# Attention in a hybrid decoder layer: turned probabilities kept in float32, each value product split by head parity onto the two halves of TensorE's columns

## The chip, the core and the metric

The kernel runs on one core of a Trainium2 chip. A core has TensorE (PE in the profile, with its loads of weights in a row of their own, PEld), VectorE (DVE), ScalarE (ACT), GpSimd (POOL) and SyncE (SP, which issues the DMAs). Tiles lie in SBUF, with 128 partitions; TensorE writes its results to PSUM, 8 banks of 2 KB a partition. The metric is the device time of one execution in microseconds, lower is better.

## What is computed

One layer of a decoder trunk on a sequence of 1024 tokens with 1024 features. The input is normalized and projected; eight heads of sparse attention (two groups of four heads of width 64, each group with one set of keys and values) and four heads of a gated delta rule work side by side, their outputs go through one projection and a residual addition, and a gated feed-forward part with a short convolution follows. The change lies in the attention. For every block of queries it forms three softmaxes and their products with values:

```python
p_cmp = masked_softmax(jnp.einsum('bqhgd,bhnd->bhgqn', qb, kc), m_cmp)      # 64 compressed keys
o_cmp = jnp.einsum('bhgqn,bhnd->bqhgd', p_cmp, vc)
...
p_sel = masked_softmax(jnp.einsum('bqhgd,bhqnd->bhgqn', qb, k_sel), m_sel[:, :, None])
o_sel = jnp.einsum('bhgqn,bhqnd->bqhgd', p_sel, v_sel)                      # selected blocks of keys
...
p_win = masked_softmax(jnp.einsum('bqhgd,bkhd->bhgqk', qb, kw), m_win)
o_win = jnp.einsum('bhgqk,bkhd->bqhgd', p_win, vw)                          # a window of 512
...
return jnp.einsum('bshc,bshcd->bshd', gate, o)                              # gated sum of the three
```

Everything is float32. The output is the layer's result after a last normalization.

## The kernel before

The program runs through four stages. `phase_in` normalizes, projects and runs the delta rule (0 to about 455 us in the trace); `phase_attend` does the attention and the part of the output projection that does not need it (to about 790); `phase_out` and `norm_second` finish the projection and the second normalization; `phase_up` and `phase_down` are the feed-forward part (from about 820).

TensorE takes float32 operands in two ways. Operands of the type float32r are rounded on writing, and one instruction multiplies them in one pass. Precision is kept by splitting a tile into a rounded high part and the rounded rest (`wh`, `wl`; `hH`, `hL`; `qh`, `ql`) and summing products of the parts in PSUM; `mm3` does so with three products. Operands of the type float32 are multiplied in full, and the trace shows two MATMUL and two LDWEIGHTS instructions for each such product. The delta rule uses these, for instance `kk_ps` (L285): 128 rows, 64 columns of weights, written by turns to partitions 0 to 63 and 64 to 127 of one PSUM tile. A transposition on TensorE takes float32 tiles and shows one instruction.

The attention works in 16 **units**: a tile of 128 queries `i` (in the order 7 to 0) and a group `g` of four heads. Each unit passes three generators. `select` forms the scores of the compressed keys (`sc_ps`) and picks the blocks. `scores` forms for each head the window scores and the scores of all earlier keys (`s_ps`, L820 and L822: high and low part of the queries against `kst`, whose 128 rows hold the high and the low part of the keys), adds masks and finds maxima on VectorE (L834), takes the exponential on ScalarE (L838) and scales by gate and sum on POOL (L854); the results are `pw` (`p_win`) and `pn` (`p_sel`). `values` (L867) sums all three value products of the unit in one PSUM tile `po`. It goes through a list of jobs: one for the 64 compressed keys, one for each 128 keys of the window (at most 5) and one for each 128 keys up to the query tile, 148 jobs over all units. A job turns the probabilities of the four heads with four transposes into the PSUM tile `pt` (L880; three buffers, shared with `og_ps`), and then:

```python
nc.scalar.activation(ph[0:kk], pt[0:kk], AF.Copy)                                       # L882: high part
...
nc.vector.tensor_tensor(out=pl, in0=pt, in1=ph.bitcast(F32), op=ALU.subtract)           # L890: the rest
nc.tensor.matmul(po, v, ph, start=False, stop=False)                                    # L891
nc.tensor.matmul(po, v, pl, start=False, stop=(n == len(jobs) - 1))                     # L892
```

The weights `v` (`K.vst`, L601) are 128 rows of keys by 128 columns, the high part of the 64 value features and beside it their low part; so `po` holds the products with the high part in partitions 0 to 63 and those with the low part in 64 to 127, 512 columns wide (four heads of 128 queries). The job of the compressed keys (L885, L886) has its 64 rows twice, the high and the low part of the probabilities below each other. At the end of a unit the two halves of `po` are copied out and added into `oT`, in which heads of even number lie in partitions 0 to 63 and of odd number in 64 to 127: for `i` under 4 one copy on ScalarE and two additions on VectorE (L897, L899), otherwise two copies on ScalarE and two additions on POOL (L904, L906). `nsa_norm` takes `oT` from there.

`K.vst` is made at the end of `phase_in`: four loads of `v_raw` from DRAM (L611), four rounding copies on ScalarE (L613) and four subtractions on POOL (L614). `K.vc` is made in `compress` with four copies on ScalarE and four subtractions on VectorE (L717, L718).

`interleave` (L92) mixes the generators of three neighbouring units and `out_gdn`, the output projection of the delta rule's part (`og_ps`, twelve products of 512 columns for a tile). That sets only the order in which the program is written: the tile framework runs it through a scheduler with a timeline of its own, which sets the order on each engine. Each engine then works through its order in turn.

Of the kernel before, what the change touches and what calls it, by code (L numbers as in the profile page):

```python
# [9 lines left out]
F32 = mybir.dt.float32  # L10
F32R = mybir.dt.float32r
BF16 = mybir.dt.bfloat16
AF = mybir.ActivationFunctionType
ALU = mybir.AluOpType
# [494 lines left out]
def phase_in(K, ctx):  # L509
# [91 lines left out]
    K.vst = vp.tile([P, NT, 2, 2, P], F32R, name="vst")  # L601
# [6 lines left out]
    vr = scr.enter_context(tc.tile_pool(name="vraw", bufs=4, side="right"))  # L608
    for j in range(4):
        raw = vr.tile([P, 2, 2, 2, 64], F32, name="v_raw", tag="v_raw")  # L610
        nc.sync.dma_start(raw.rearrange("p t b g d -> p t (b g d)"), K.d_v[:, 2 * j:2 * j + 2, :])  # L611
        d = slice(2 * j, 2 * j + 2)
        nc.scalar.activation(K.vst[:, d, :, :, 0:64], raw, AF.Copy)  # L613
        nc.gpsimd.tensor_tensor(out=K.vst[:, d, :, :, 64:128], in0=raw, in1=K.vst[:, d, :, :, 0:64].bitcast(F32),  # L614
                                op=ALU.subtract)
# [46 lines left out]
def compress(K, which, pool):  # L662
# [47 lines left out]
    else:  # L710
        for h in range(2):
            vp = K.pp.tile([64, 64], F32, name="vc_ps", tag="proj")
            for j in range(2):
                nc.tensor.matmul(vp, x[:, j, 64 * h:64 * h + 64], w2[:, j, :], start=(j == 0), stop=(j == 1))

            for d in (slice(0, 64), slice(64, 128)):
                nc.scalar.activation(K.vc[d, h, 0:64], vp, AF.Copy, scale=0.5)  # L717
                nc.vector.scalar_tensor_tensor(out=K.vc[d, h, 64:128], in0=vp, scalar=0.5,  # L718
                                               in1=K.vc[0:64, h, 0:64].bitcast(F32), op0=ALU.mult, op1=ALU.subtract)
# [147 lines left out]
def values(K, i, g, U):  # L867

    nc = K.nc
    pc, pw, pn, lo = U.pc, U.pw, U.pn, U.lo  # L870
    po = K.p_o.tile([P, 4, P], F32, name="po", tag="po")
# [5 lines left out]
    for n, (src, v, kk) in enumerate(jobs):  # L877
# [3 lines left out]
        ph = K.apl.tile([P, 4, P], F32R, name="ph", tag="ph", bufs=3)  # L881
        nc.scalar.activation(ph[0:kk], pt[0:kk], AF.Copy)  # L882
        if n == 0:

            nc.vector.tensor_tensor(out=ph[kk:P], in0=pt[0:kk], in1=ph[0:kk].bitcast(F32), op=ALU.subtract)  # L885
            nc.tensor.matmul(po, v, ph, start=True, stop=False)  # L886
            yield
            continue
        pl = K.apl.tile([P, 4, P], F32R, name="pl", tag="pl", bufs=3)
        nc.vector.tensor_tensor(out=pl, in0=pt, in1=ph.bitcast(F32), op=ALU.subtract)  # L890
        nc.tensor.matmul(po, v, ph, start=False, stop=False)  # L891
        nc.tensor.matmul(po, v, pl, start=False, stop=(n == len(jobs) - 1))  # L892
        yield

    if i < 4:
        lo_ = K.apl.tile([64, 4, P], F32, name="po_s", tag="po_s", bufs=1)
        nc.scalar.activation(lo_, po[64:128], AF.Copy)  # L897
        for par in range(2):
            nc.vector.tensor_tensor(out=U.oT[64 * par:64 * par + 64, 2 * g:2 * g + 2, :], in0=po[0:64, par::2, :],  # L899
                                    in1=lo_[:, par::2, :], op=ALU.add)  # L900
        return
    hh = K.apl.tile([64, 2, 4, P], F32, name="po_s", tag="po_s", bufs=1)
    for j in range(2):
        nc.scalar.activation(hh[:, j], po[64 * j:64 * j + 64], AF.Copy)  # L904
    for par in range(2):
        nc.gpsimd.tensor_tensor(out=U.oT[64 * par:64 * par + 64, 2 * g:2 * g + 2, :], in0=hh[:, 0, par::2, :],  # L906
                                in1=hh[:, 1, par::2, :], op=ALU.add)
# [512 lines left out]
def open_common(K, ctx):  # L1420
# [22 lines left out]
    K.vc = cp.tile([P, 2, P], F32R, name="vc")  # L1443
# [103 lines left out]
```

## Time and profile before

| | us |
|---|---|
| median of 3 runs | 1500.02 (1499.13 to 1500.04) |
| the profiled execution, its own time | 1502.3 |
| its span, first to last instruction | 1500.5 |
| first transpose of probabilities to last value product | 502.8 to 790.4 |

The profile is of one execution. Its times are microseconds, ns where said. A busy share is the time in which an engine has at least one instruction under way; matmuls overlap each other, so it says little of how full TensorE is. A row of the timeline is a start, a duration, engine and line, operation, the tile written and the tiles read, the form (rows by columns of the weights, then partitions by columns of the moving tile) and how many like it stand in a row; the duration of a row of several runs from the first start to the last end. A releaser ("<-") is what an idle engine was waiting for.

### The profile page before, as it was taken

To read this page: it belongs to the slowest core of one execution; us is meant where nothing else is said; L and a number is where in the kernel's file an instruction comes from. 1 tells how busy PE (TensorE), PEld (TensorE's weight loads), DVE (VectorE), ACT (ScalarE), POOL (GpSimd) and SP (SyncE) were. 2 spreads that over 40 slices of the span, in tenths; PEclk is the share of its full clock that TensorE was granted. 3 is DMA by queue.
4 is the path that set the end of the run, shared out by engine and by line. 5 is a ranking of instruction groups with operands and counts; after the bars stand their busy time and mean duration, and the time that the engine had idled before them with its cause. 6 is when DMAs were issued, how large, how long until landed. Compare 5 with 4: busy or idle time off the path is not lost.

```text
span 1500.5 us, 21074 instructions
## 1 busy us (share of the span) xinstructions
PE 1420.9 (95%) x7260; PEld 1163.8 (78%) x7260; DVE 1153.7 (77%) x2222; ACT 723.3 (48%) x1405; POOL 575.3 (38%) x567
## 2 busy tenths in 40 slices
PE   8998899999989999989998979999999999989997
PEld 8876677787877777777787858888888888778886
DVE  5768997886335788898975797888888888687656
ACT  7443343232233566788865544444444445333333
POOL 3355433344352245466563541111111112364444
PEclk9999999999999999999999989999999999999999
DMA  6245352444366543132215112323222235773333
GB/s 234 87 156 177 107 169 72 125 121 150 93 219 173 161 138 112 58 85 52 55 64 200 40 70 105 105 105 106 105 94 98 97 105 194 268 267 87 103 106 147
DMA packets 106059, 188.04 MB, mean 125 GB/s; under 512 B 17216, under 2 KB 52064, under 8 KB 105952
## 3 DMA queue, kind: packets, MB, share of 16 engines
q1 hardware_dynamic: 105952, 186.69, 38.5%
q8 instruction: 57, 0.93, 0.3%
q14 instruction: 50, 0.41, 0.1%
HBM read 135.00 MB, written 51.66 MB: 124 GB/s over the span
## 4 chain that ended last, share of the span: by engine, by line
PE 64%; DVE 19%; DMA 6%; ACT 4%; issue 4%; POOL 2%; SPq 1%; DVEq 0%; ACTq 0%; POOLq 0%
PE up_ps L1130 27%; PE dn_ps L1328 11%; PE proj_ps L128 3%; PE proj_ps L126 3%; PE proj_ps L127 3%; DVE cv_acc L465 3%; PE pt L880 2%; DVE pl L890 2%; PE po L892 1%; DVE zb L350 1%; PE po L891 1%; DVE ztmp L348 1%; PE s_ps L820 1%; PE s_ps L415 1%; DMA d_x<-og 1%
## 5 line engine op out<-in xcount | busy, mean ns | idle before, releaser
L1328 PE MATMUL dn_ps<-d_op 128*128 128x512 f32 x924 | 211.4, 390 | 5.7 <-DVE d_op L1322 3.8
L1328 PEld LDWEIGHTS dn_ps<-d_op 128*128 128x128 f32 x924 | 173.0, 188 | 43.6 <-DVE d_op L1322 5.0
L128 PE MATMUL proj_ps<-hH,w_l 128*128 128x512 f32 x384 | 158.3, 412 | 6.6 <-POOL w_l L118 6.6
L126 PE MATMUL proj_ps<-hH,w_h 128*128 128x512 f32 x384 | 156.2, 408 | 5.0 <-ACT cv_acc L463 3.2
L127 PE MATMUL proj_ps<-hL,w_h 128*128 128x512 f32 x384 | 155.3, 405 | 0.1
L1320 POOL TENSOR_TENSOR d_op<-a_raw,d_op 128x1024 fp32r<-128x1024 f32 (+1 forms) x42 | 104.7, 2496 | 123.0 <-ACT d_op L1319 105.6
L1130 PE MATMUL up_ps<-th,op_h 128*128 128x512 f32 x336 | 133.5, 398 | 7.1 <-ACT op_h L1154 7.1
L1130 PE MATMUL up_ps<-th,op_l 128*128 128x512 f32 x336 | 133.6, 398 | 3.6 <-DVE op_l L1156 3.6
L1130 PE MATMUL up_ps<-tl,op_h 128*128 128x512 f32 x336 | 133.3, 397 | 0.0
L118 POOL TENSOR_TENSOR w_l<-w_raw,w_h 128x1024 fp32r<-128x1024 f32 (+2 forms) x46 | 110.1, 2398 | 46.1 <-ACT w_h L116 44.5
L1322 DVE TENSOR_TENSOR d_op<-b,d_op 128x1024 fp32r<-128x1024 f32 (+1 forms) x42 | 80.8, 1928 | 48.5 <-ACT d_op L1321 42.1
L1130 PE MATMUL up_ps<-dl,op_h 128*128 128x512 f32 x288 | 113.8, 395 | 0.0
L1130 PE MATMUL up_ps<-dh,op_h 128*128 128x512 f32 x288 | 112.6, 395 | 1.0 <-ACT acc L167 1.0
L1130 PE MATMUL up_ps<-dh,op_l 128*128 128x512 f32 x288 | 110.5, 394 | 0.0
L882 ACT ACTIVATE ph<-pt 128x512 fp32r<-128x512 f32 (+1 forms) x148 | 85.3, 591 | 49.1 <-PE pt L880 41.3
L1242 DVE SCALAR_TENSOR_TENSOR ga<-f_g,vec,ga 128x1024 f32<-128x1024 f32 x44 | 89.3, 2029 | 16.9 <-ACT ga L1240 16.3
L890 DVE TENSOR_TENSOR pl<-pt,ph 128x512 fp32r<-128x512 f32 x132 | 89.5, 683 | 9.1 <-ACT ph L882 8.6
L128 PEld LDWEIGHTS proj_ps<-hH,w_l 128*128 128x128 f32 x384 | 74.6, 194 | 26.9 <-POOL w_l L118 10.6
L1154 ACT ACTIVATE op_h<-w_raw 128x1024 fp32r<-128x1024 f32 (+1 forms) x64 | 59.0, 923 | 74.8 <-PE up_ps L1130 69.7
L1319 ACT ACTIVATE d_op<-a_raw 128x1024 fp32r<-128x1024 f32 (+1 forms) x42 | 41.4, 988 | 108.7 <-PE dn_ps L1328 53.8
L1175 POOL MEMSET f_u<- 128x2 f32 x22 | 2.2, 100 | 234.0 <-DVE acc L1242 233.1
L126 PEld LDWEIGHTS proj_ps<-hH,w_h 128*128 128x128 f32 x384 | 74.6, 195 | 21.2 <-ACT cv_acc L463 4.9
(343 smaller groups left out, 3654.6 us busy)
## 6 DMA issues: line engine op xcount, KB each, us to landing
w_raw<-in_w_up_dram SPq DMA_DIRECT2D x44, 512.0 KB, 3.2
a_raw<-d_a SPq DMA_DIRECT2D x35, 512.0 KB, 3.6
w_raw<-in_w_gdn_dram SPq DMA_DIRECT2D x24, 512.0 KB, 3.5
d_a<-ga SPq DMA_DIRECT2D x44, 256.0 KB, 2.0
b<-in_w_down_dram SPq DMA_DIRECT2D x20, 512.0 KB, 6.9
d_a<-so SPq DMA_DIRECT2D x33, 256.0 KB, 2.0
qT<-d_q SPq DMA_DIRECT2D x32, 256.0 KB, 4.8
mg<-d_mix SPq DMA_DIRECT2D x16, 512.0 KB, 3.7
```

The source lines that it names most:

```text
L118: (low or nc.gpsimd).tensor_tensor(out=wl, in0=raw, in1=wh.bitcast(F32), op=ALU.subtract)
L126: nc.tensor.matmul(out, ah, bh, start=(i == 0), stop=False)
L127: nc.tensor.matmul(out, ah, bl, start=False, stop=False)
L128: nc.tensor.matmul(out, al, bh, start=False, stop=(i == n - 1))
L882: nc.scalar.activation(ph[0:kk], pt[0:kk], AF.Copy)
L890: nc.vector.tensor_tensor(out=pl, in0=pt, in1=ph.bitcast(F32), op=ALU.subtract)
L1130: mm = lambda a, b, start, stop: nc.tensor.matmul(out, a, b, start=start, stop=stop, skip_group_check=not first)
L1154: nc.scalar.activation(h, src, AF.Copy)
L1242: nc.vector.scalar_tensor_tensor(out=a, in0=raw[:, j:j + SEQ], scalar=tap(j), in1=a, op0=ALU.mult, op1=ALU.add)
L1320: nc.gpsimd.tensor_tensor(out=al, in0=raw, in1=ah.bitcast(F32), op=ALU.subtract)
L1322: nc.vector.tensor_tensor(out=bl, in0=b[js.start], in1=bh.bitcast(F32), op=ALU.subtract)
L1328: one = lambda a, b, start, stop: nc.tensor.matmul(ps, a, b, start=start, stop=stop, skip_group_check=not first)
```

## The change

The probabilities are no longer split. `pt` is copied once to a float32 tile `pT`, by VectorE in every fourth job (`n % 4 == 3`) and by ScalarE in the others. The values stay float32 as well: `K.vst` is loaded from DRAM by one DMA with nothing done to it, `K.vc` takes one copy a group. `po` becomes a tile of 256 columns: the heads of even number are multiplied into its partitions 0 to 63, those of odd number into 64 to 127, each with the same 64 columns of values as weights, so that it has the layout of `oT` and is copied there by one instruction on ScalarE.

```diff
-    K.vst = vp.tile([P, NT, 2, 2, P], F32R, name="vst")
+    K.vst = vp.tile([P, NT, 2, 2, 64], F32, name="vst")
+    nc.sync.dma_start(K.vst.rearrange("p t b g d -> p t (b g d)"), K.d_v)
...
-    vr = scr.enter_context(tc.tile_pool(name="vraw", bufs=4, side="right"))
-    for j in range(4):
-        raw = vr.tile([P, 2, 2, 2, 64], F32, name="v_raw", tag="v_raw")
-        nc.sync.dma_start(raw.rearrange("p t b g d -> p t (b g d)"), K.d_v[:, 2 * j:2 * j + 2, :])
-        d = slice(2 * j, 2 * j + 2)
-        nc.scalar.activation(K.vst[:, d, :, :, 0:64], raw, AF.Copy)
-        nc.gpsimd.tensor_tensor(out=K.vst[:, d, :, :, 64:128], in0=raw, in1=K.vst[:, d, :, :, 0:64].bitcast(F32),
-                                op=ALU.subtract)
...
-            for d in (slice(0, 64), slice(64, 128)):
-                nc.scalar.activation(K.vc[d, h, 0:64], vp, AF.Copy, scale=0.5)
-                nc.vector.scalar_tensor_tensor(out=K.vc[d, h, 64:128], in0=vp, scalar=0.5,
-                                               in1=K.vc[0:64, h, 0:64].bitcast(F32), op0=ALU.mult, op1=ALU.subtract)
+            nc.scalar.activation(K.vc[:, h], vp, AF.Copy, scale=0.5)
...
-    po = K.p_o.tile([P, 4, P], F32, name="po", tag="po")
+    po = K.p_o.tile([P, 2, P], F32, name="po", tag="po")
...
-        ph = K.apl.tile([P, 4, P], F32R, name="ph", tag="ph", bufs=3)
-        nc.scalar.activation(ph[0:kk], pt[0:kk], AF.Copy)
-        if n == 0:
-
-            nc.vector.tensor_tensor(out=ph[kk:P], in0=pt[0:kk], in1=ph[0:kk].bitcast(F32), op=ALU.subtract)
-            nc.tensor.matmul(po, v, ph, start=True, stop=False)
-            yield
-            continue
-        pl = K.apl.tile([P, 4, P], F32R, name="pl", tag="pl", bufs=3)
-        nc.vector.tensor_tensor(out=pl, in0=pt, in1=ph.bitcast(F32), op=ALU.subtract)
-        nc.tensor.matmul(po, v, ph, start=False, stop=False)
-        nc.tensor.matmul(po, v, pl, start=False, stop=(n == len(jobs) - 1))
+        pT = K.apl.tile([P, 4, P], F32, name="pT", tag="pT", bufs=4)
+        if n % 4 == 3:
+            nc.vector.tensor_copy(pT[0:kk], pt[0:kk])
+        else:
+            nc.scalar.activation(pT[0:kk], pt[0:kk], AF.Copy)
+        for par in range(2):
+            nc.tensor.matmul(po[64 * par:64 * par + 64], v, pT[0:kk, par::2], start=(n == 0), stop=(n == len(jobs) - 1))
         yield
-
-    if i < 4:
-        lo_ = K.apl.tile([64, 4, P], F32, name="po_s", tag="po_s", bufs=1)
...
+    nc.scalar.activation(U.oT[:, 2 * g:2 * g + 2, :], po, AF.Copy)
...
-    K.vc = cp.tile([P, 2, P], F32R, name="vc")
+    K.vc = cp.tile([64, 2, 64], F32, name="vc")
```

The scheduler makes a new order. On TensorE in the first third of the stage (`pt` are transposes of four heads, `po` value products, `s_ps` scores of the next unit), before:

```order
L880 MATMUL pt<-ident,p_win 128x128 x8
L891 MATMUL po<-ph,vst 128x512
L892 MATMUL po<-pl,vst 128x512
L880 MATMUL pt<-ident,p_sel 128x128 x4
L891 MATMUL po<-ph,vst 128x512
L820 MATMUL s_ps<-kst_4413,qT 128x384
L822 MATMUL s_ps<-kst_4413,qT 128x384
L820 MATMUL s_ps<-kst_4413,qT 128x256
L822 MATMUL s_ps<-kst_4413,qT 128x256
L892 MATMUL po<-pl,vst 128x512
```

and in the changed kernel at the same place:

```order
L872 MATMUL pt<-ident,p_win 128x128 x8
L879 MATMUL po<-pT,vst 64x256 x2
L872 MATMUL pt<-ident,p_sel 128x128 x4
L879 MATMUL po<-pT,vst 64x256 x2
L872 MATMUL pt<-ident,p_sel 128x128 x4
L809 MATMUL s_ps<-kst_4407,qT 128x384
L811 MATMUL s_ps<-kst_4407,qT 128x384
L879 MATMUL po<-pT,vst 64x256 x2
L872 MATMUL pt<-ident,p_sel 128x128 x4
```

The two products of a job, which stood apart with scores between them, now stand together, between transposes or scores of full width. Over all units the 296 value products stand in 129 places.

On ScalarE at the end of `phase_in` (`q_h` is the rounded part of the queries, `w_h` of weights, `wq` the delta rule's output), before:

```order
L643 ACTIVATE q_h<-proj_ps 128x512
L116 ACTIVATE w_h<-w_raw 128x1024 x2
L643 ACTIVATE q_h<-proj_ps 128x512
L613 ACTIVATE vst<-v_raw 128x8x64 x4
L643 ACTIVATE q_h<-proj_ps 128x512
```

and changed:

```order
L636 ACTIVATE q_h<-proj_ps 128x512 x2
L443 ACTIVATE wq<-zT 128x4x128
L636 ACTIVATE q_h<-proj_ps 128x512
L116 ACTIVATE w_h<-w_raw 128x1024 x2
L636 ACTIVATE q_h<-proj_ps 128x512
```

The copies into `vst` between the last two `q_h` are gone; on SP the one load of `vst` stands some eight DMAs earlier than the four loads of `v_raw` stood.

## Rows read from the trace of the kernel before

**Rows 1.** The page's busy time: us (share of the span) x instructions.
```profile
PE 1420.9 (95%) x7260; PEld 1163.8 (78%) x7260; DVE 1153.7 (77%) x2222; ACT 723.3 (48%) x1405; POOL 575.3 (38%) x567
```
**Rows 2.** Windows: length; busy us (count) of PE, PEld, DVE, ACT, POOL; PEclk; DMA.
```profile
502.80:790.40 287.60, 267.96 (x1591) 222.73 (x1589) 247.14 (x808) 211.32 (x537) 149.44 (x217) 0.99 0.30 86
```
**Rows 3.** PE's groups in that stretch: count | busy us, mean ns | idle before.
```profile
L892 PE MATMUL po<-pl,vst 128*128 128x512 f32 x132 | 57.5, 436 | 7.1 <-DVE pl L890 6.8
L891 PE MATMUL po<-ph,vst 128*128 128x512 f32 x132 | 55.8, 423 | 2.0 <-ACT ph L882 2.0
L880 PE MATMUL pt<-ident,p_sel 128*128 128x128 f32 x288 | 44.9, 277 | 1.8 <-DVE og L952 1.8
L880 PE MATMUL pt<-ident,p_win 128*128 128x128 f32 x240 | 36.4, 274 | 5.8 <-DVE pl L890 2.9 <-DVE ph L885 1.6 <-DVE og L952 1.3
L126 PE MATMUL og_ps<-w_h,mg 128*128 128x512 f32 x72 | 29.3, 407 | 0.1
...
L820 PE MATMUL s_ps<-kst,qT 128*128 128x512 f32 x48 | 22.0, 459 | 1.0 <-DVE nmax L834 1.0
L820 PE MATMUL s_ps<-kst,qT 128*128 128x384 f32 x49 | 19.2, 391 | 0.0
...
L820 PE MATMUL s_ps<-kst,qT 128*128 128x256 f32 x50 | 15.7, 320 | 0.0
```
**Rows 4.** Timeline of PE around 654 us: start, duration, line, tiles, form, count.
```profile
654.41 0.40 PE L892 MATMUL po<-pl,vst 128*128 128x512 f32 x1
654.64 0.39 PE L891 MATMUL po<-ph,vst 128*128 128x512 f32 x1
654.87 0.60 PE L880 MATMUL pt<-ident,p_sel 128*128 128x128 f32 x4
655.23 0.30 PE L820 MATMUL s_ps<-kst,qT 128*128 128x128 f32 x1
```
**Rows 5.** Timeline of PE around 109 us, in the delta rule.
```profile
109.21 0.39 PE L127 MATMUL proj_ps<-hL,w_h 128*128 128x512 f32 x1
109.53 1.09 PE L285 MATMUL kk_ps<-kq 128*64 128x128 f32 x16
110.55 0.50 PE L128 MATMUL proj_ps<-hH,w_l 128*128 128x512 f32 x1
110.89 0.40 PE L126 MATMUL proj_ps<-hH,w_h 128*128 128x512 f32 x1
```
**Rows 6.** Timeline of PE around 301 us (`ot_ps` are transposes).
```profile
300.35 0.60 PE L437 MATMUL ot_ps<-ident,vv 128*128 128x128 f32 x4
300.88 0.44 PE L285 MATMUL kk_ps<-kq 128*64 128x128 f32 x4
301.25 0.66 PE L437 MATMUL ot_ps<-ident,vv 128*128 128x128 f32 x4
```
**Rows 7.** By tile: ns shortest/median/longest, first and last start in us.
```profile
L270 PE MATMUL nd_ps<-ug,cst x8: 590/592/697, 80.6 to 287.0; 128*128 128x512 f32 x8
...
L285 PE MATMUL kk_ps<-kq x128: 272/273/324, 109.5 to 302.4; 128*64 128x128 f32 x128
```
**Rows 8.** PE's waits from 502.8 to 790.4 us, the first and the last: total, times, longest.
```profile
PE po L892 <- DVE pl L890: 6.8, 8, 1.9
...
PE po L886 <- DVE oT L899: 0.2, 1, 0.2
```
**Rows 9.** The page's groups of `ph` and `pl`: busy us, mean ns | idle before.
```profile
L882 ACT ACTIVATE ph<-pt 128x512 fp32r<-128x512 f32 (+1 forms) x148 | 85.3, 591 | 49.1 <-PE pt L880 41.3
...
L890 DVE TENSOR_TENSOR pl<-pt,ph 128x512 fp32r<-128x512 f32 x132 | 89.5, 683 | 9.1 <-ACT ph L882 8.6
```
**Rows 10.** The chain that ended last, at 438 us: start, duration.
```profile
438.64 5.63 DMA v_raw<-d_v
```
**Rows 11.** PE's waits from 455 to 810 us, one row.
```profile
PE sc_ps L744 <- DMA qT<-d_q: 1.6, 1, 1.6
```
**Rows 12.** Timeline of PE at 420 us.
```profile
420.88 0.79 PE L126 MATMUL proj_ps<-hH,w_h 128*128 128x512 f32 x1 [1.58 <-DVE vc L718]
```

More of the change, by code (lines that the diff above doesn't have):

```diff
@@ L880, in values @@
             nc.tensor.transpose(pt[0:kk, h, :], src[h], K.ident)
-        ph = K.apl.tile([P, 4, P], F32R, name="ph", tag="ph", bufs=3)
-        nc.scalar.activation(ph[0:kk], pt[0:kk], AF.Copy)
-        if n == 0:
-            nc.vector.tensor_tensor(out=ph[kk:P], in0=pt[0:kk], in1=ph[0:kk].bitcast(F32), op=ALU.subtract)
-            nc.tensor.matmul(po, v, ph, start=True, stop=False)
-            yield
-            continue
-        pl = K.apl.tile([P, 4, P], F32R, name="pl", tag="pl", bufs=3)
-        nc.vector.tensor_tensor(out=pl, in0=pt, in1=ph.bitcast(F32), op=ALU.subtract)
-        nc.tensor.matmul(po, v, ph, start=False, stop=False)
-        nc.tensor.matmul(po, v, pl, start=False, stop=(n == len(jobs) - 1))
-        yield
-    if i < 4:
-        lo_ = K.apl.tile([64, 4, P], F32, name="po_s", tag="po_s", bufs=1)
[L897 to L907, printed above, removed]
+        pT = K.apl.tile([P, 4, P], F32, name="pT", tag="pT", bufs=4)
[5 more added lines that the diff above has]
+            nc.tensor.matmul(po[64 * par:64 * par + 64], v, pT[0:kk, par::2], start=(n == 0), stop=(n == len(jobs) - 1))
+        yield
+    nc.scalar.activation(U.oT[:, 2 * g:2 * g + 2, :], po, AF.Copy)
 def nsa_norm(K, i, o):
```

## The prediction

> **What bounds the kernel now.** By the page's busy shares PE is busy 95% of the span [rows 1]. A busy share does not say how full PE is, so I cut out the stage that the change touches, from the first probability transpose (502.8) to the last value product (790.4): 287.6 us, in which PE is busy 268 us and VectorE 247 us [rows 2]. The question is whether PE's own work fills the stage or whether PE waits for VectorE's `pl`. I counted PE's instructions there by shape [rows 3] and took from the timeline how far apart they start when nothing is in the way: a rounded (float32r) product of 512 columns takes its place for 0.23 us (the two value products start at 654.41 and 654.64), a transpose for 0.11 us (four last 0.60, a single one 0.27, so three steps are 0.33), and the step to the next operation costs next to nothing [rows 4]. Then, in us: 592 transposes (528 in the rows, 64 of `pc` by the code) x 0.11 = 65; 280 value products (132 `pl`, 132 `ph` and 16 of the compressed values by the code) x 0.23 = 64; 217 products of `og` (three rows of 72 or 73, of which one stands) x 0.23 = 50; score products, each row having a twin for the low part, 96 x 0.23 = 22, 98 at 384/512 of that = 17, 100 at half = 11; about 200 small ones at 0.11 or less, 19. That is 249 of 287.6. **PE is 87% full there, and 38 us are left for waits**, of which the waits list names 18.6 us in nine rows, the longest for `pl` [rows 8]. So VectorE can give back at most 38 us; anything over that would have to come off PE.
>
> **What the change takes away.** VectorE loses 132 `pl` at 683 ns [rows 9], 90 us, 16 half-height ones and 16 final additions. It gets the copy of every fourth job (n = 3, 7, 11 in a unit: 30 in all), at most 0.68 each like `pl`, the nearest row that reads as much from PSUM: 20 us. So its 247 fall to under 177. ScalarE loses those 30 copies and the ones of `po_s`. Neither ends this stage afterwards. What PE gains is waits only: nearly all of the 18.6 us named are for `pl`, `ph` or for an `og` addition that stands behind `pl` on VectorE, so I let 18 go and keep 20 of the 38 (late first score maxima, ScalarE behind a weight's DMA, the clock at 0.99 [rows 2]). Ends for what stays: 0 and 38.
>
> **What the change puts on PE.** Each job had two rounded products of 512 columns, 0.46 us. Now it has two true float32 products of 256 columns, into partitions 0 to 63 and 64 to 127 of `po`. Three terms, each from work of the same kind elsewhere in this trace.
> First, the rate. A float32 product appears as two passes (the trace counts 16 where the order has 8). A pass of 512 columns lasts 592 ns and one of 128 lasts 273 [rows 7]; (592-273)/384 = 0.83 ns a column. So a pass of 256 columns takes 0.21 us, and the four of a job, one after the other, would take 0.85.
> Second, whether the halves run together. `kk_ps` is the row to go by: float32, 64 columns of weights, the same two halves in turn. From the end of L127 (109.60) to the end of `kk_ps` (110.62) are 1.02 us for 16 passes of 128 columns [rows 5]; at 0.107 each they would need 1.71. They run in pairs: 8 x 0.107 = 0.86, and 0.16 is left over. So a job is two paired steps, 0.43 us, against 0.46 (0.23 in the first job of a unit): 148 x 0.43 = 64 against 64. **The arithmetic is a draw.**
> Third, the switch. The 0.16 is what PE pays to go from full width to halves: `kk_ps` starts 0.32 after L127, not 0.23, and its first passes last up to 324 ns, not 273 [rows 5, 7]. Coming back, L128 ends 0.43 after `kk_ps` instead of 0.23: 0.20 [rows 5]. Between transposes it is the same: from the end of the first four (300.95) to the end of the next four (301.91) are 0.96 us, for 0.21 of paired passes and 0.44 of transposes; 0.31 for both switches, 0.16 in and 0.15 out [rows 6]. Rounded products and transposes follow each other without it [rows 4]. So the price hangs on how often the value products stand alone in PE's order. Counted there, the 296 stand in 129 separate places (103 of them one job), 94 with a transpose behind them, 35 with something else. 129 x 0.16 + 94 x 0.15 + 35 x 0.20 = 42 us. Five jobs have their halves apart, each alone on PE: 5 x 0.43 = 2. In 12 places a product of the 64-row compressed values meets one of 128 rows, another geometry: 12 x 0.15 = 2.
> Sum on PE: 249 - 64 + 64 + 42 + 2 + 2 = 295 us of work, **already 7 more than the whole stage takes now**, and with 20 us of waits 315: +27.
>
> **A rule against it.** `kk_ps` shows no loading of weights between its steps after the first [rows 5, 7]. The Trainium skill (TensorE: Matmul & The Clock Gate, Part 3, The mechanism) says that a weight load overlaps running products only when the row groups differ; here both halves use all rows, so each step would show its load. A load that shows is 324 - 273 = 51 ns [rows 7], one more per job: 148 x 0.05 = 7 us. I leave it out of the sum, as the row speaks against it, and keep it as a rival.
>
> **Before and after the stage.** The chain ahead of it runs through the load of `v_raw` (438.6 to 444.3) [rows 10], whose four copies stand ahead of the last `q_h` on ScalarE; PE then waits 1.6 us for the queries that come of it [rows 11]. Both go. The one load that replaces four is as large as they are together and stands earlier on SP, ahead of the writes of `d_q`, so these can land later by as much as one such load: between -5 and +5, I take -2, near the wait that the row shows. The eight small operations on `vc` become two copies; PE waited 1.6 us for the last of them [rows 12]: -1. At the end one copy of `po` stands for a copy and two additions: -1. Elsewhere no instruction changes. Together -4.
>
> **The sum.** 27 - 4 = +23 on the profiled execution's 1502.3, which stands 2.3 over the median of the runs: 1523, and since a few switches fall into waits that are there anyway, **1522**. With no waits left and -7 outside the stage it is 1500; with 38 us of waits and nothing gained outside, 1545.
>
> **The rivals.**
> *The halves don't run together* (0.09). `kk_ps` starts fresh sums, while `po` adds up over a whole unit in one bank; should that, or the order of the passes, keep the halves apart, each job takes 0.85 instead of 0.43: 148 x 0.43 = +63 us, 1585. Against it: the pairs of the only like row [rows 5].
> *Every load shows* (0.07): 1522 + 7 = 1529, by the rule above; on the same side.
> *The waits were VectorE's alone and cover the switches* (0.14, the other side). If all 38 us came from VectorE's queue they go, and if half of the blocks come up before their `pT` has landed, the switch lies in time that PE would lose anyway, say 20 us of the 42: 295 - 20 = 275, -13 in the stage and -4 outside: 1483. It decides where the waits that stay and the switches that show come to under 38 us together. For it: VectorE is busy for 86% of the stage [rows 2]. Against it: between a job's last transpose and its products the new order has some 4 us of PE work (the median, at the prices above), and the copy needs 0.6 [rows 9], so a block seldom waits and its switch shows.
> *A draw* (0.10): no waits to speak of, all switches: 295 to 299 in the stage, 7 to 12 more, less 7 to 10 outside: 1497 to 1503.
>
> **How the numbers follow.** The forecast has 0.60 and its own range of 1503 to 1545; the loads' rival lies within it. Under it stand the draw (0.10) and the faster case (0.14), over it the halves' case (0.09). A range that leaves out no more than two in ten has to take in the draw and the near part of the faster case: 1494 to 1546. What a measurement of this kernel can tell from no change is about 0.2%, 3 us: faster 0.14, same 0.10, slower 0.76.
>
> **What would show it.** In the trace of after: value products in groups of four passes, two starting together and the next two 0.21 us later (if all four are 0.21 apart, the first rival); the operation behind each group ending 0.15 to 0.20 us later than in its usual place; the stage from the first transpose to the last value product 300 to 330 us long although VectorE's busy time in it falls under 177; PE's waits for VectorE mostly gone. I am wrong if the stage gets shorter than 287 us although the switches show as priced (then the waits were mis-sized, or the switches lie in them), or if the groups show no switch at all. PE's granted clock should stay at its upper level of 2.4 GHz, as now (0.99) [rows 2].

## The result: 1.2% slower, and where it went

The changed kernel takes 1520.0 us (median of four runs, 1515.7 to 1521.1), the kernel before 1500.0 beside it: a ratio of 1.0123, 95% interval 1.0097 to 1.0149. The forecast was 1522. The profiled execution has a span of 1518.9 us, 18.4 more than before.

The page's busy time of after, to be held against [rows 1]:

```profile
PE 1448.1 (95%) x7572; PEld 1135.7 (75%) x7572; DVE 1088.8 (72%) x2084; ACT 695.0 (46%) x1361; POOL 555.7 (37%) x547
```

VectorE lost 65 us of busy time, ScalarE 28, and PE gained 27. The stage again runs from the first probability transpose to the last value product; its row answers [rows 2], with length, then the busy us (and count) of PE, PEld, DVE, ACT, POOL, and the granted clock:

```profile
495.70:796.20 300.50, 296.99 (x1904) 200.76 (x1902) 180.51 (x678) 186.85 (x499) 137.16 (x203) 0.99 0.29 82
```

PE idles in 300.5 - 297.0 = 3.5 us of it; before it idled in 287.6 - 268.0 = 19.6. So PE is busy for 29 us more and idle for 16 us less: +12.9. Busy time is not work, though: a product shows as busy for 0.40 us and takes its place for 0.23 [rows 4], so short waits hide in it. By the forecast's prices for each operation PE had 249 us of work before and has 295 now. On that scale its work grew by 46 us, and its waits fell from 38 us to 5.5 (300.5 - 295). Its groups in that stretch (count | busy us, mean ns | idle before), for [rows 3]:

```profile
L879 PE MATMUL po<-pT,vst 128*64 128x256 f32 x528 | 87.2, 404 | 0.0
L872 PE MATMUL pt<-ident,p_sel 128*128 128x128 f32 x288 | 47.7, 285 | 0.0
L872 PE MATMUL pt<-ident,p_win 128*128 128x128 f32 x240 | 39.1, 282 | 0.3 <-DVE pT L875 0.3
...
L809 PE MATMUL s_ps<-kst,qT 128*128 128x384 f32 x50 | 20.0, 401 | 3.2 <-DVE nmax L823 3.2
...
L879 PE MATMUL po<-pT,vc 64*64 64x256 f32 x64 | 10.4, 402 | 0.0
```

In [rows 3] the value products had 7.1 and 2.0 us of idle time before them and the transposes 7.6; now they have none to speak of. The whole list of PE's waits in the stage, nine rows in [rows 8], has two, and the first is a single late score maximum:

```profile
PE s_ps L809 <- DVE nmax L823: 3.2, 1, 3.2
PE pt L872 <- DVE pT L875: 0.3, 1, 0.3
```

What a value product costs is on PE's timeline (start, duration, line, tiles, form, count), for [rows 4]:

```profile
602.91 0.23 PE L813 MATMUL s_ps<-masks 128*128 128x128 bf16 x1
603.07 0.65 PE L879 MATMUL po<-pT,vst 128*64 128x256 f32 x4
603.66 0.50 PE L127 MATMUL og_ps<-w_l,mg 128*128 128x512 f32 x1
```

The mask product ends at 603.14, the group of four passes at 603.72: 0.58 us, which is two paired steps of 0.215 and 0.15 for the way in. L127 ends 0.44 later, where such a product's usual step is 0.23: 0.20 to 0.21 for the way back. Over the stage the median of the 103 groups of four is 0.58, and a transpose behind a group ends after 0.26 (usual step 0.11; 0.15 for the way back).

The span falls into three pieces, which the experiments move one by one. The rows below "after" are the kernels of the experiments, which are described further down. Places are stretches of value products in column halves in PE's order, so a kernel without halves has none; what lies behind the stage is counted to the end of the span.

| profiled kernel | median of runs | stage begins | stage | PE idle in it | VectorE busy in it | places | behind it |
|---|---|---|---|---|---|---|---|
| before | 1500.0 | 502.8 | 287.6 | 19.6 | 247 | none | 710.1 |
| after | 1520.0 | 495.7 | 300.5 | 3.5 | 181 | 129 | 722.7 |
| one half of the columns | 1567.8 | 495.1 | 353.8 | 0.0 | 179 | 124 | 718.8 |
| full width | 1537.5 | 494.8 | 317.7 | 1.6 | 179 | none | 720.5 |
| four jobs together | 1488.8 | 497.0 | 276.4 | 3.4 | 178 | 50 | 713.8 |
| late turn | 1516.7 | 494.8 | 301.3 | 4.1 | 181 | 129 | 719.3 |
| two jobs together | 1503.1 | 495.6 | 288.7 | 3.6 | 182 | 91 | 720.2 |
| VectorE busy | 1519.7 | 493.2 | 301.7 | 8.4 | 256 | 110 | 721.3 |
| values split again | 1516.1 | 493.0 | 300.5 | 2.8 | 181 | 129 | 722.1 |
| eight jobs together | 1489.3 | 498.3 | 280.7 | 4.4 | 176 | 46 | 709.4 |
| two-step turn | 1526.6 | 497.2 | 307.7 | 7.4 | 243 | 132 | 720.3 |
| four jobs, two-step turn | 1512.5 | 497.8 | 303.0 | 17.7 | 241 | 46 | 710.7 |
| before without low parts | 1494.6 | 498.1 | 274.3 | 12.1 | 178 | none | 720.2 |

So the 18.4 us are -7.1 ahead of the stage, +12.9 in it and +12.6 behind it. The last piece was not foreseen. PE's timeline of after at the end of the stage, with idle time before an operation and what ended it in brackets:

```profile
795.52 0.65 PE L879 MATMUL po<-pT,vst 128*64 128x256 f32 x4
...
798.73 0.38 PE L892 MATMUL nrm_ps<-ones,sq 128*128 128x1 f32 x2 [1.42 <-POOL sq L889]
800.46 0.49 PE L899 MATMUL rs_ps<-dg,ones 128*128 128x128 f32 x2 [1.35 <-POOL dg L896]
806.63 1.09 PE L147 MATMUL nt_ps<-ident,acc 128*128 128x128 f32 x4 [5.69 <-DVE acc L170]
808.34 0.80 PE L126 MATMUL out_ps<-w_h,mh 128*128 128x512 f32 x1 [0.62 <-ACT mh L1011]
808.93 0.63 PE L127 MATMUL out_ps<-w_l,mh 128*128 128x512 f32 x1
```

and of before, the same place:

```profile
789.92 0.50 PE L892 MATMUL po<-pl,vst 128*128 128x512 f32 x1
793.28 0.51 PE L126 MATMUL out_ps<-w_h,mh 128*128 128x512 f32 x1 [2.86 <-ACT mh L1037]
...
798.19 0.28 PE L918 MATMUL nrm_ps<-ones,sq 128*128 128x1 f32 x2
```

Before, the output projection's products (`out_ps`) began 2.9 us after the last value product and covered the norms (`nrm_ps`, `rs_ps`) of the last rows. After, the two norms and the turning of the first normalised rows (`nt_ps`) stand ahead of `out_ps` in PE's order, each waits with nothing beside it, and `out_ps` begins 12.2 us after the end of the last value product. Its first products end 0.42 us apart instead of 0.23; the windows say why (columns as above, the clock is the third number from the end):

```profile
796.20:836.00 39.80, 30.68 (x140) 24.78 (x140) 18.07 (x33) 16.57 (x29) 9.79 (x15) 0.87 0.42 152
...
802.40:812.60 10.20, 5.35 (x14) 4.12 (x15) 4.33 (x10) 5.42 (x10) 4.27 (x9) 0.50 0.74 269
```

The granted clock stood at its lower level, 1.2 GHz, for 10.2 us, from inside the wait of 5.7 us on; before, it stood there for 3.4 us at this place. When the first product of the feed-forward part (`up_ps`) starts, 40.2 us after the stage against 31.6 before, 8.6 of the 12.6 us are lost. The other 4.0 come later and were not followed up.

### The profile page after: what moved, and what is told of

It is laid out like the page before. It is cut to its first block, busy times and chain, and to the rows that moved or that the text cites. A ratio compares the mean times of both kernels' runs of the same rounds, so it can differ in the third digit from the quotient of the medians.

```text
span 1518.9 us, 21429 instructions
## 1 busy us (share of the span) xinstructions
PE 1448.1 (95%) x7572; PEld 1135.7 (75%) x7572; DVE 1088.8 (72%) x2084; ACT 695.0 (46%) x1361; POOL 555.7 (37%) x547
## 4 chain that ended last, share of the span: by engine, by line
PE 70%; DVE 15%; DMA 5%; issue 3%; ACT 3%; POOL 2%; SPq 1%; DVEq 0%; ACTq 0%; POOLq 0%
PE up_ps L1104 27%; PE dn_ps L1302 10%; PE po L879 6%; PE pt L872 5%; DVE cv_acc L465 4%; PE proj_ps L128 2%; PE s_ps L809 2%; PE proj_ps L126 2%; PE proj_ps L127 2%; PE s_ps L811 2%; DVE ztmp L348 2%; DVE zb L350 2%; PE og_ps L126 1%; PE og_ps L128 1%; PE og_ps L127 1%
## 5 line engine op out<-in xcount | busy, mean ns | idle before, releaser
L128 PE MATMUL proj_ps<-hH,w_l 128*128 128x512 f32 x384 | 155.2, 404 | 7.3 <-POOL w_l L118 7.3
L127 PE MATMUL proj_ps<-hL,w_h 128*128 128x512 f32 x384 | 152.7, 398 | 0.1
L877 ACT ACTIVATE pT<-pt 128x512 f32<-128x512 f32 (+1 forms) x118 | 67.7, 589 | 57.1 <-PE pt L872 55.2
L465 DVE SCALAR_TENSOR_TENSOR cv_acc<-cv_raw,vec,cv_acc 128x512 f32<-128x512 f32 x72 | 76.4, 1061 | 18.4 <-ACT cv_acc L463 16.2
```

Of the source, the lines that this page charges most:

```text
L127: nc.tensor.matmul(out, ah, bl, start=False, stop=False)
L128: nc.tensor.matmul(out, al, bh, start=False, stop=(i == n - 1))
L465: nc.vector.scalar_tensor_tensor(out=acc, in0=raw[:, j:j + 512], scalar=tap(j), in1=acc, op0=ALU.mult, op1=ALU.add)
```

## The experiments

All edits are to the changed kernel, except that of the run without low parts, which is to the kernel before.

**Do the halves run together?** One 512-wide product per job, in one half of the columns.

```diff
-    po = K.p_o.tile([P, 2, P], F32, name="po", tag="po")
+    po = K.p_o.tile([64, 4, P], F32, name="po", tag="po")
...
-        for par in range(2):
-            nc.tensor.matmul(po[64 * par:64 * par + 64], v, pT[0:kk, par::2], ...)
+        nc.tensor.matmul(po, v, pT[0:kk], ...)
...
+    for par in range(2):
+        nc.scalar.activation(U.oT[64 * par:64 * par + 64, 2 * g:2 * g + 2, :], po[:, par::2], AF.Copy)
```

> The four turned heads of a job go through one 512-wide product into 64 rows of the result, so all of it uses the same half of the array's columns; two copies by ScalarE put the parities where they belong. Same products, same number of switches (124 places, 129 in the changed kernel). Theory: the halves of the changed kernel run together, a pass of 256 being 0.21 us for two. Then 144 groups of four passes grow from 0.43 to about 0.85 us, and as there are 304 pairs of passes at 0.21 us, the time is 1520 + 63 = 1583 us. Rival: the halves do not run together and the pairs of starts in the trace are only how it is drawn; then 1520 us stays within 5.

Measured: 1567.8 us, ratio 1.046 (1.0444 to 1.0476) to before, 47.8 more than the changed kernel, where the theory had 63; the stage is 53.3 longer. PE's timeline:

```profile
518.28 0.40 PE L811 MATMUL s_ps<-kst,qT 128*128 128x512 f32 x1
518.61 1.07 PE L878 MATMUL po<-pT,vst 128*64 128x512 f32 x2
519.61 0.50 PE L809 MATMUL s_ps<-kst,qT 128*128 128x512 f32 x1
```

From the end of L811 (518.68) to the end of the two passes (519.68) are 1.00 us, where the changed kernel needs 0.58: 0.42 more for each of the 143 jobs whose halves stood together, 60 us. The stage gives some 7 us of that back: 3.5 of idling, 1.6 by five places fewer, the rest was not followed up. The halves run together; without that the change would have cost about 68 us.

**What is the price of changing between whole array and halves?** The values twice side by side, one 512-wide product on all 128 columns.

```diff
-    K.vst = vp.tile([P, NT, 2, 2, 64], F32, name="vst")
+    K.vst = vp.tile([P, NT, 2, 2, P], F32, name="vst")
...
-        for par in range(2):
-            nc.tensor.matmul(po[64 * par:64 * par + 64], v, pT[0:kk, par::2], ...)
+        nc.tensor.matmul(po, v, pT, ...)
...
+    for par in range(2):
+        d = slice(64 * par, 64 * par + 64)
+        nc.scalar.activation(U.oT[d, 2 * g:2 * g + 2, :], po[d, par::2], AF.Copy)
```

> Values stand twice side by side, so that each job is one 512-wide float32 product on all 128 columns, all four heads at once, of which half of the rows is thrown away; the compressed values get 64 rows of zero. No change between whole array and column halves is left. Theory: with no halves there is no price for the change of geometry, 129 places at 0.31 to 0.35 us = 40 to 45 us, while the passes cost the 63 us of the kernel with all in one half. Then 1583 - 42 = 1541 us, and the two kernels differ by 40 us. Rival: the extra 0.15 and 0.20 us behind a group belong to something else, the loading of float32 weights or the wait for the copy: then both kernels are within 8 us of each other, near 1580 us.

Measured: 1537.5 us, ratio 1.0263 (1.0235 to 1.0291). PE's timeline:

```profile
517.13 0.40 PE L815 MATMUL s_ps<-kst,qT 128*128 128x512 f32 x1
517.37 1.02 PE L884 MATMUL po<-pT,vst 128*128 128x512 f32 x2
517.83 0.80 PE L813 MATMUL s_ps<-kst,qT 128*128 128x512 f32 x1
```

L815 ends at 517.53, the two passes at 518.39 (0.86, no way in), L813 at 518.63 (0.24, no way back). The same float32 products in the same copies show no extra time, so the 0.15 and 0.20 belong to the change of geometry. Between this kernel and the one with one half the stage differs by 36.1 us, the runs by 30.3; 124 places at 0.31 would be 38, and the theory had 40. This is also the first part of the change alone (float32, not split): without the split by parity it would have cost 37 us instead of 20.

**Fewer places.** The value products of G jobs are held back and issued together.

```diff
+    held, done, G = [], 0, 4
     for n, (src, v, kk) in enumerate(jobs):
...
-        for par in range(2):
-            nc.tensor.matmul(po[64 * par:64 * par + 64], v, pT[0:kk, par::2], ...)
+        held.append((v, pT, kk))
+        if n % G == G - 1 or n == len(jobs) - 1:
+            for v, pT, kk in held[::-1]:
+                done += 1
+                for par in range(2):
+                    nc.tensor.matmul(po[64 * par:64 * par + 64], v, pT[0:kk, par::2], ...)
+            held.clear()
```

With G = 4 and eight buffers of `pT`:

> The value products of four jobs are held back and issued together (in reverse order), eight buffers for the turned probabilities instead of four. The places where TensorE goes to the halves and back fall from 129 to 50. Theory: each place costs 0.31 to 0.35 us, so 79 fewer give 24 to 28 us back, about 1494 us. Rival: the cost hangs on each product (its float32 weights), and then the time stays at 1520 within 4; a second rival: holding back makes TensorE wait for the turned copies at the end of each group, and then the gain is under 12 us, with PE waits for ACT and DVE on the line of the value products.

Measured: 1488.8 us, 31 less than the changed kernel and **faster than the kernel before: ratio 0.993 (0.9909 to 0.9951)**. The row of windows for its stage, and one group in PE's timeline:

```profile
497.00:773.40 276.40, 272.96 (x1901) 205.91 (x1899) 177.67 (x675) 185.50 (x499) 137.58 (x201) 1.00 0.31 89
```

```profile
545.54 0.60 PE L873 MATMUL pt<-ident,p_sel 128*128 128x128 f32 x4
546.06 1.95 PE L884 MATMUL po<-pT,vst 128*64 128x256 f32 x16
```

Sixteen passes take 1.87 us from the end of the transposes (546.14 to 548.01): eight pairs at 0.215 and 0.15 once. The stage is 24.1 us shorter for 79 places fewer, 0.31 us each. Behind the stage it gains 8.9 more, and it starts 1.3 later.

With G = 2 and the four buffers of the changed kernel:

> As the run with four jobs held back, but two: 91 places where TensorE goes to the column halves and back (129 in the changed kernel, 50 with four jobs held). Theory: the stage shrinks by 38 places at 0.31 us = 12 us, as it shrank by 24 us with 79 places fewer; behind the stage between 0 and 9 us more, as the order of the projection falls. So 1520 - 12 to 21 = 1499 to 1508 us. Rival: what helped with four jobs was the deeper buffering (eight buffers of turned probabilities), which is not in this one (four, as in the changed kernel): then 1518 to 1522 us.

Measured: 1503.1 us, ratio 1.0022 (1.0012 to 1.0033). The stage is 11.8 us shorter for 38 places, 0.31 us each again, so it is the places and not the buffers; the piece behind the stage gained 2.5.

With G = 8 and twelve buffers:

> Up to eight jobs held back, twelve buffers: 46 places of switching (50 with four jobs). Theory: 4 places fewer give 1 us: 1487 to 1489 us, the same as with four jobs. Rival: groups of sixteen or more passes starve the copies: the transposes of the next group come later, ScalarE and VectorE idle and then TensorE waits for the first turned copy: 1490 to 1500 us.

Measured: 1489.3 us, ratio 0.9931 (0.9914 to 0.9948), as with four. The pieces are not the same, though: with four places fewer the stage is 4.3 us longer than with four jobs, 1.0 of it idle, and the piece behind it 4.4 shorter. So 0.31 us a place is borne out by two and by four jobs, and not by eight; why the stage is longer there was not followed up.

**The end of the stage.** In the projection, the transposes of the first half's normalised rows are issued behind the last product of the rows of the next two tiles.

```diff
-        for b, tiles in HALVES:
+        last = None
+        for b, tiles in ((0, (7, 6, 5, 4, 3, 2)), (1, (7, 6, 5, 4)), (0, (1, 0))):
...
             if b:
-                norm_transpose(K, tiles, ...)
+                with tc.issue_after(last.ins):
+                    norm_transpose(K, tiles, ...)
```

> Attention as in the changed kernel; in the projection that follows, the transposes of the first half's normalised rows are put behind the projection of the rows of the next tiles, as TensorE had them in the kernel before. Theory: of the 12 us that the changed kernel loses behind the attention, 6 to 9 are the wait of 5.7 us for the first normalised rows and the half clock of 10.2 us that follows it; 1520 - 6 to 9 = 1511 to 1514 us. Rival: the loss follows from the later end of the attention and shifts to the next wait: 1520 within 3.

Measured: 1516.7 us, ratio 1.0119 (1.0101 to 1.0137), 3.4 less than the changed kernel. The two kernels' runs overlap (1514.8 to 1519.5 and 1515.7 to 1521.1), and so do their ratios to the kernel before, so the gain is not clear of noise, and the theory's 6 to 9 us did not come. PE's waits behind the stage:

```profile
PE out_ps L126 <- ACT mh L1013: 4.3, 1, 4.3
PE nrm_ps L893 <- POOL sq L890: 1.4, 1, 1.4
PE rs_ps L900 <- POOL dg L897: 1.4, 1, 1.4
```

The wait for the first normalised rows is gone, but `out_ps` then waits 4.3 us for its own rows, since the two norms still stand ahead of it and nothing covers them. The wait was mostly moved, as the rival had it. The table shows the same from the other side. Before and the kernels with four, eight and four two-step jobs have 709 to 714 us behind the stage, and in them PE idles for 0.9 to 2.9 us in the 12 us that follow the last value product. All other kernels looked at there have 719 to 723 and idle 7 to 9 us. So most of the +12.6 goes with the order in which PE meets the last norms. No run changed that order alone, so this is read from the orders that came about and not shown by an experiment.

**Why did PE's waits go?** First VectorE's load alone: one subtraction more per job, into a buffer that nobody reads.

```diff
+        lo_ = K.apl.tile([P, 4, P], F32, name="lo_", tag="lo_", bufs=3)
+        nc.vector.tensor_tensor(out=lo_[0:kk], in0=pt[0:kk], in1=pT[0:kk], op=ALU.subtract)
```

> The changed kernel, and for each job VectorE also subtracts the turned copy from the turned probabilities into a buffer that nobody reads, as it had to for the low parts before: 144 more instructions of about 0.69 us, 95 us more on VectorE in the stage (181 to about 276 us, of 300). Theory: that TensorE's waits in the stage fell from 38 to about 5 us is VectorE's relief, so they come back: 20 to 40 us more, 1540 to 1560 us, with waits of TensorE for VectorE in its list. Rival: the waits went because the value products no longer need a second and a third buffer, or because TensorE itself became slower and everything else got ahead of it: then 1520 to 1530 us.

Measured: 1519.7 us, ratio 1.0132 (1.0117 to 1.0148), no change. The order of PE came out with 110 places instead of 129, worth -6 us; idle time rose by 5:

```profile
493.20:794.90 301.70, 293.34 (x1907) 202.70 (x1905) 256.04 (x827) 186.78 (x499) 137.34 (x203) 0.99 0.28 82
```

VectorE is busy for 85% of the stage, as it was before (86%), yet PE idles in 8.4 us and not in 19.6. The theory that the relief of VectorE by itself removed the waits, with its 20 to 40 us, falls. Next, VectorE put back on the path of the product:

```diff
-        if n % 4 == 3:
-            nc.vector.tensor_copy(pT[0:kk], pt[0:kk])
-        else:
-            nc.scalar.activation(pT[0:kk], pt[0:kk], AF.Copy)
+        ph = K.apl.tile([P, 4, P], F32, name="ph", tag="ph", bufs=3)
+        nc.scalar.activation(ph[0:kk], pt[0:kk], AF.Copy)
+        nc.vector.tensor_tensor(out=pT[0:kk], in0=pt[0:kk], in1=ph[0:kk], op=ALU.max)
```

> The changed kernel, but each turned job passes as before through two engines ahead of its product: ScalarE copies it out, then VectorE forms the larger of the turned job and its copy (the same numbers), and the product takes that. VectorE has again an instruction of about 0.69 us for each of 144 jobs, now on the path of the product; 132 switches. Theory: the 29 us of waits in the stage of the kernel before came from this chain in front of the product, not from VectorE's load alone (with the load alone, 256 us of 301, the time did not move): then 10 to 25 us more, 1530 to 1545 us, with TensorE's waits on the value products for VectorE. Rival: TensorE with the switches is so slow that four turned buffers cover the chain as well: 1518 to 1526 us.

Measured: 1526.6 us, ratio 1.018 (1.0159 to 1.0201): 6.5 us more than the changed kernel, just past the rival's 1526 and short of the theory's 1530. The stage is 7.2 us longer, of it 3.9 idle and 0.9 by three places more. The same edit where PE has less to do, four jobs together:

> Four jobs held back, eight buffers, and the turn in two steps over ScalarE and VectorE as in the run beside it. TensorE's need in the stage is about 270 us and VectorE has about 256 to 275. Theory that TensorE's pace hid VectorE: the waits come back when TensorE is faster, 10 us or more: 1498 to 1510 us against 1489. Theory that the chain's place ahead of the product is what costs: held-back products come late anyway, so the chain is hidden: 1487 to 1492 us.

Measured: 1512.5 us, ratio 1.009 (1.0064 to 1.0117), 23.7 more than the kernel with four jobs alone and above the first theory's 1498 to 1510; the second theory, which had 1487 to 1492, falls. The row of windows for its stage, and the first four of PE's waits there:

```profile
497.80:800.80 303.00, 285.27 (x1903) 209.51 (x1901) 240.68 (x795) 202.06 (x529) 137.66 (x201) 0.97 0.29 82
```

```profile
PE pt L873 <- DVE og L932: 4.0, 3, 1.6
PE pt L873 <- DVE pT L877: 3.9, 7, 1.6
PE s_ps L809 <- ACT rs L907: 3.3, 1, 3.3
PE po L883 <- DVE pT L877: 2.8, 4, 1.1
```

PE idles in 17.7 us, and the granted clock averages 0.97 against 1.00, up to 9 us more. These are the waits of the kernel before again: transposes and value products behind VectorE's `og` and the second step of the turn. The same work on VectorE costs 4 us of idling where PE was busy for 297 us without it, and 14 where it was busy for 273 (with four jobs alone); the stage grew by 7.2 and by 26.6 us. So what the two-step turn costs hangs on how much PE has to do besides. VectorE's load alone does not decide it. By the forecast's prices, less 0.31 us for each place fewer, VectorE's busy time is 0.89 of PE's work in the kernel with VectorE busy (256 beside 289 us) and also in the one with four jobs and the two-step turn (241 beside 269); what this leaves for waits in the stage is 13 us in the first and 34 in the second. The load together with VectorE's place ahead of the product brought the waits back only where PE had less to do; the load alone was not tried there.

Last, in the kernel before, the low parts left out and the high parts multiplied twice:

```diff
-        pl = K.apl.tile([P, 4, P], F32R, name="pl", tag="pl", bufs=3)
-        nc.vector.tensor_tensor(out=pl, in0=pt, in1=ph.bitcast(F32), op=ALU.subtract)
...
-        nc.tensor.matmul(po, v, pl, start=False, stop=(n == len(jobs) - 1))
+        nc.tensor.matmul(po, v, ph, start=False, stop=(n == len(jobs) - 1))
```

> The kernel before, without the subtraction that forms the low part of the turned probabilities; the second product of a job takes the high part once more, so that TensorE has the same products (the low parts are left out of the result and the high ones come twice). VectorE loses 128 instructions of 0.69 us, 88 us of its 247 in the stage. Theory: the 29 us by which TensorE waits in the stage of the kernel before hang on VectorE and its low parts: 15 to 25 us less, 1475 to 1485 us. Rival: they hang on the copies by ScalarE and on the small buffers: 1495 to 1500 us.

Measured: 1494.6 us, ratio 0.9969 (0.9952 to 0.9985): the theory's 1475 to 1485 did not come, and the rival's 1495 is close. The stage loses 13.3 us, of which 10 are given back behind it (720.2 instead of 710.1, the order of the norms again). The stage:

```profile
498.10:772.40 274.30, 262.15 (x1588) 222.44 (x1587) 178.48 (x676) 207.89 (x537) 149.25 (x217) 0.98 0.31 90
```

Even with VectorE at 178 us PE still idles in 12.1, 5.5 of them behind `og` on VectorE and 4.0 behind score maxima; beside 249 us of work the stage leaves 25 for waits. The changed kernel has as little on VectorE and 5.5 us of waits. So the relief of VectorE, taken alone, removed 13 us of waits, and the whole change 33. What removed the other 20 was not settled: PE's longer work is one candidate, and the four buffers of `pT` against three of `ph` are another, which weren't tried.

**Ahead of the stage.** The values loaded, copied and subtracted in four parts as before.

```diff
-    nc.sync.dma_start(K.vst.rearrange("p t b g d -> p t (b g d)"), K.d_v)
+    for j in range(4):
+        raw = vr.tile([P, 2, 2, 2, 64], F32, name="v_raw", tag="v_raw")
+        nc.sync.dma_start(raw.rearrange("p t b g d -> p t (b g d)"), K.d_v[:, 2 * j:2 * j + 2, :])
+        d = slice(2 * j, 2 * j + 2)
+        nc.scalar.activation(K.vst[:, d], raw, AF.Copy)
+        nc.gpsimd.tensor_tensor(out=raw, in0=raw, in1=K.vst[:, d], op=ALU.subtract)
```

> The changed kernel, but the values come as before in four loads, with ScalarE's copies and GpSimd's subtractions of the low parts (which nobody uses). Theory: the 7 us by which the stage begins earlier, where I had forecast 2, come from these loads and splits at the front: 1520 + 5 to 7 = 1525 to 1527 us with the first probability transpose near 502. Rival: they come from the order of the first score products, since VectorE and the probability buffers are freer in the first units: then 1520 to 1522 us and the first transpose near 496.

Measured: 1516.1 us, ratio 1.0106 (1.0091 to 1.0122): not slower, and the stage begins at 493.0. The loads are not what the earlier start comes from. Windows of before and of after up to the stage:

```profile
440.00:502.80 62.80, 59.16 (x262) 47.25 (x261) 32.95 (x118) 24.71 (x60) 24.59 (x23) 0.95 0.69 201
459.00:463.00 4.00, 4.00 (x12) 3.15 (x11) 0.00 (x0) 0.00 (x0) 0.00 (x0) 0.57 1.14 219
```

```profile
440.00:495.70 55.70, 53.49 (x248) 42.44 (x247) 31.53 (x114) 22.48 (x55) 19.11 (x17) 1.00 0.69 200
```

Before ran this stretch at 0.95 of the clock, with a dip to the lower level from 459 on, right behind the wait of [rows 11]; after ran it at 1.00. That is some 3 of the 7 us. Another part is order: of the products into `s_ps` after has 374 in the stage and before 370, so four moved behind its beginning. The kernel without low parts, whose code ahead of the stage is that of before, began its stage at 498.1, so 5 us of this start move with the order and the clock alone. How they share it is not shown: the full-width kernel had a granted clock of 0.94 in this stretch and began its stage at 494.8.

## Why the prediction was right, and where its steps were not

The sign was right, and the mechanism on PE is shown. The time was right too (1522 against 1520.0), but that it came so close is luck: two terms were off and partly cancel. On the profiled executions the stage came out 14.1 us better than the sum had it (+12.9 for +27), the rest 9.5 worse (+5.5 for -4).

*The rate, the pairs, the draw.* Right. In the group at 603.07 two passes start together, and the next two end 0.215 us after them (they start 0.27 later, not 0.21). Two paired steps take 0.43 us, and the kernel with one half shows the 0.85 of the first rival. That rival falls.

*The switch.* Right, to the hundredth: 0.15 in, 0.15 out to a transpose, 0.20 out to a 512-wide product. The kernels with two and four jobs held back confirm 0.31 per place over the stage, and the full-width kernel that it is the geometry.

*The loads.* The second rival falls: eight pairs take 1.87 us, 0.215 a pair after the way in, so no load of weights shows although PEld has one for each pass. The rule that I weighed in the Trainium skill (TensorE: Matmul & The Clock Gate, Part 3, The mechanism), that loads overlap running products only where row groups differ, does not hold for these two column halves. The same section also lets a load into a background weight buffer run ahead, which I had left out; no run here tells whether that is what hides these loads.

*PE's own work.* 295 us forecast. The row's 297.0 us of busy time does not prove it, since before 268 busy us stood against 249 of work; but the stage of 300.5 leaves little room above it, and its largest new term, the switches, is borne out place by place.

*The waits.* This is the term that was mis-sized in the stage. I let 18 of 38 us go and kept 20; on the same scale 5.5 stayed, which is the whole miss of the stage; its 300.5 us lie at the very edge of the 300 to 330 that were named as a sign. I split the waits by whom they were for and kept those not of `pl`, as if each would stay when PE has more to do. The runs show that they don't: the same two-step turn added 7.2 us to a stage of 300 us and 26.6 to one of 276. VectorE's load alone does not set them either, and the full cause stays open.

*VectorE.* Forecast under 177 us, measured 180.5. The copies cost what was taken, 0.69 us (shortest, median, longest ns, from the view by tile):

```profile
L875 DVE COPY pT<-pt x30: 676/690/694, 499.2 to 774.2; 128x512 f32<-128x512 f32 x30
```

*Before the stage.* -3 forecast (-2 for the load, -1 for `vc`), -7.1 measured, and not for the reason given: with the old loads it begins no later.

*Behind the stage.* "Elsewhere no instruction changes" was true of the count, not of PE's order. I had read the order where value products stand, not at the stage's last rows, where the norms had moved ahead of `out_ps`. That is +12.6 where I had -1; without it the time would have been near 1507.

*The faster rival.* Its first half came true, the waits went. Its second did not: no switch lay in a wait. The kernel with four jobs together shows what it would have taken: fewer places.

*A draw.* In the stage this rival was nearer than the forecast: no waits to speak of and all switches, 295 to 299 us, against 300.5 measured and 315 forecast. What it had wrong is the rest, 7 to 10 us less outside where 5.5 more came.

## What to carry to other kernels

A product that uses half of the columns pays at each place where PE's order changes to it and back (0.31 us here), not for each product: count the places before splitting, and gather the products. Waits are not a fixed sum: here work added to the engine that waits ate most of them (46 us more work by the forecast's prices, a stage 12.9 us longer), and the same work put on the other engine cost 7 us or 27, by how much the first had to do. Where an order is planned again, read its seams, the last rows of the stage above all, as closely as the changed lines.

## What the chip showed that I had not expected

Idle time can be paid twice. Amid waits of 1.42, 1.35 and 5.69 us the granted clock of after was 0.50 for 10.2 us, and behind its one wait of 3.2 us in the stage for 3.4 us. The kernel with one half, whose PE never idled in 353.8 us, kept 1.00 throughout the stage, and the kernel with four jobs and the two-step turn lost up to 9 us by the clock beside its 17.7 us of idling. It does not follow each time: the kernels with two and with four jobs together idled for 3.6 and 3.4 us of the stage, in shorter waits, and kept 1.00.
